# The 3 MB table of the relative bias written ahead of the values' projection instead of in the attention's set-up

## The chip, the cores and the metric

One core of one Trainium2 chip runs one decoder layer for a prompt group (2048 tokens) and a sample group (8 sequences, one token each). The metric is device microseconds of one execution; the kernel before takes 2285.19 us (median of 3 runs, 2283.89 to 2285.52). TensorE does matrix products, ScalarE and VectorE elementwise work, GpSimd some of it; SyncE (SP) does nothing but issue transfers. In this kernel transfers are issued by SP (they run on DMA queue 1) and by ScalarE (queue 10).

## The reference, cut to what matters

```python
h    = x * (1 + scale) + shift                    # scale, shift, gate from silu(c) @ w_ada
u_s, z_s, q, k, v, z_a, g_s, g_a = split(h @ w_in)
b_s  = (glu(gelu(S5(u_s))) * silu(z_s)) @ w_branch_s
s    = q . k / 8 + rel_bias[bucket(distance)]     # 16 heads, window of 128, masked outside
o    = softmax(s with a sink per head) @ v
b_a  = (o * silu(z_a)) @ w_branch_a
m    = sigmoid(g_s) * b_s + sigmoid(g_a) * b_a
y    = layer_norm(alpha * x + gate * (m @ w_out))
```

The bias depends only on the head and on the distance of query and key (0 to 128). The same formula runs for the 8 sample tokens against a cache of 128 keys and values, which is also returned, shifted by one.

## The kernel before, in words

Activations lie transposed, channels on the partitions, tokens along the free axis in five chunks of 512, 512, 512, 256 and 264 columns (the last holds the 8 sample tokens). A float32 product is made of three matmuls on split operands (high with high, high with low, low with high; L78). Weight columns come 128 at a time: SP loads them into `wst` (L55), ScalarE makes `whi` (L58), VectorE `wlo` (L59). A job is one such block times five chunks; each chunk is accumulated over 8 slices of 128 channels in one of three PSUM buffers `acc`, then copied out through one of two buffers with the tag `ev` and stored to DRAM.

The program runs in stages. Phase 1 (from about 20 to 332 us of the profiled span) makes u and the tables of the state-space branch, then in a pool `p1z` the first two blocks of z_a (the copies-out store to `zaP` by SP, L550) with the gate's small matmuls between them, and last `v_proj` (L648): the values, tokens on the partitions, in 17 tiles of up to 128 tokens. Each tile is 24 matmuls of 256 columns into an `acc` buffer (L665), a copy by ScalarE to `vt` in an `ev` buffer (L668), and a store to `vD` issued by ScalarE (L670). So three PSUM buffers and two `ev` buffers stand between TensorE and the stores. After it SP issues two copies of the sample caches to the outputs, about 1 MB each (`out_sk`, `out_sv`, L645). Phase 2 runs the scan of the state-space branch beside projection jobs.

Phase 3 begins near 903 us with `attn_setup` (L883), beside a projection job (`zr`, stored to `zsD` by ScalarE, L586 and L587). It builds the bias: a one-hot matrix times `rel_bias` gives 129 values for each of 16 heads (`pr`), VectorE puts them into `fr`, sixteen partitions of 384 columns that are -1e30 outside, and one transfer writes `fr` 128 times over into `biasD` in DRAM, 16 x 128 rows of 1536 bytes, 3072 KB (L895). Read back with a row length of 383, that is the band of biases of a block of queries (L1002). The set-up then does the whole attention of the sample tokens: scores, softmax (L864; the exponentials on ScalarE are L876 and L877), a transpose of the probabilities `t1s` (L940), products with the cached values (L954). The loop over the prompt's blocks (`attn_blocks`) follows, and is the first to read `biasD`. Phases 4 and 5 are the remaining products and the layer norm.

The code is written in stages, but a scheduler of the framework places each instruction on its engine's list; each engine then works its list in order. Every transfer tells its landing by one of eight semaphores in turn (`DMAHW0` to `DMAHW7` in the orders below), so that the ninth transfer waits for the first before it is issued.

Of the kernel before, what the change touches and what calls it, by code (L numbers as in the profile page):

```python
# [9 lines left out]
F32 = mybir.dt.float32  # L10
# [29 lines left out]
class Trunk:  # L40
# [576 lines left out]
    def phase1(self, ues, up):  # L617
        nc, I = self.nc, self.I
        w = I["w_in"][0]
        with ExitStack() as ses:  # L620
            self.sps = self.pool(ses, "sp1", 2, PSUM)
            with ues, ExitStack() as es:
                self.prp = self.pool(es, "prep")
                side = self.ssm_prep()
                jobs = []
                for m in range(1, 8):
                    b, e, f = self.u_job(up, m)
                    if m == 1:
                        def b(b=b, e=e):
                            b()  # L630
                            e(ORD[0], self.early)
                    jobs.append((self.cols(w, U0 + m * 128), e, b, f))
                self.products(jobs, self.X, self.cols(w, ZA0), self.every(3, side), first=ORD[1:])
                for _ in side:
                    pass
            with ExitStack() as es:
                p = self.pool(es, "p1z", 2)
                side = self.gate(p)
                self.products([self.za_job(m) for m in range(2)], self.X, self.cols(w, ZA0 + 256), self.every(2, side))
                for _ in side:  # L640
                    pass
                self.v_proj(p)
        for nm, src in (("sk", "cache_swa_k"), ("sv", "cache_swa_v")):
            self.tc.keep_in_program_order(
                nc.sync.dma_start(self.O[nm][0, :, 0:127].rearrange("b w g d -> b w (g d)"),  # L645
                                  I[src][0, :, 1:128].rearrange("b w g d -> b w (g d)")))
# [233 lines left out]
        for h in range(nh):  # L880
            v.tensor_scalar(t1[:, h, kw], t1[:, h, kw], den[:, h:h + 1], None, op0=OP.mult)

    def attn_setup(self, p, pp):  # L883
        nc, I = self.nc, self.I
        oh = p.tile([32, 129], F32, name="oh")
        nc.sync.dma_start(oh, I["c_onehot"])
        rb = p.tile([32, 16], F32, name="rb")
        nc.sync.dma_start(rb, I["rel_bias"])
        pr = pp.tile([16, 129], F32, name="pt", bufs=2)
        nc.tensor.matmul(pr, rb, oh, start=True, stop=True)  # L890
        fr = p.tile([16, 384], F32, name="fr")

        nc.vector.memset(fr, NEG)
        nc.vector.tensor_scalar(fr[:, 127:256], pr, 8.0, None, op0=OP.mult)
        nc.sync.dma_start(self.biasD.rearrange("h (r l) -> h r l", l=384), fr[:, None, :].to_broadcast([16, 128, 384]))  # L895

        rr = p.tile([32, NS, 16], F32, name="rr")
        nc.vector.tensor_copy(rr, rb[:, None, :].to_broadcast([32, NS, 16]))
# [532 lines left out]
```

## Time and profile before

| | |
|---|---|
| median of 3 runs | 2285.19 us |
| the profiled execution | 2281.77 us, its span 2280.0 us |
| TensorE busy | 2228.8 us, 98% |
| VectorE, ScalarE, GpSimd busy | 1464.8, 786.9, 349.7 us |
| DMA | 317.98 MB, 139 GB/s over the span |

The span runs from the first instruction to the last; all times within it count from its start. Busy shares are means over stages with different limits, so each stage is read by itself: which wait ends last there. L12 is line 12 of the kernel before.

### The profile page before, as it was taken

The numbers are of one execution on the slowest core, as the hardware profiler recorded it, in microseconds if no ns is written. First come the engines' busy times: TensorE is split into PE (matmuls) and PEld (weight loads), VectorE is DVE, ScalarE is ACT, GpSimd is POOL, SyncE is SP. The second block draws the span as 40 slices with busy tenths as digits, with TensorE's granted clock in tenths as the row PEclk, the third lists the DMA queues.
The fourth block names the chain that finished last, engine by engine and source line by source line (L and its number), as shares of the span: only waits on it lengthen the run. The fifth ranks groups of instructions, "written<-read, shape, count | busy, mean of one in ns | idle before, by whom it ended". The sixth has DMA issues, their size and how long they took to land.

```text
span 2280.0 us, 35059 instructions
## 1 busy us (share of the span) xinstructions
PE 2228.8 (98%) x12571; PEld 1904.1 (84%) x12571; DVE 1464.8 (64%) x3576; ACT 786.9 (35%) x1700; POOL 349.7 (15%) x420
## 2 busy tenths in 40 slices
PE   7999999999999999999999999999999999999998
PEld 5888798888888888788888888887877888888886
DVE  4896219998888883168998888546345115124887
ACT  3411213332111111167777667554234114112100
POOL 1100001111111111000000000014441000222232
PEclk9999999999999999999999999999999999999999
DMA  9344523334443343743334343477338447667431
GB/s 298 104 143 141 181 97 113 112 118 119 119 121 114 112 124 112 131 130 113 108 116 140 101 121 105 123 168 199 107 102 273 129 115 231 201 187 227 147 113 66
DMA packets 387502, 317.98 MB, mean 139 GB/s; under 512 B 89334, under 2 KB 331406, under 8 KB 385743
## 3 DMA queue, kind: packets, MB, share of 16 engines
q1 hardware_dynamic: 349616, 260.28, 40.3%
q10 hardware_dynamic: 37712, 55.47, 7.2%
q8 instruction: 99, 1.62, 0.3%
q14 instruction: 75, 0.61, 0.1%
HBM read 195.24 MB, written 122.63 MB: 139 GB/s over the span
## 4 chain that ended last, share of the span: by engine, by line
PE 80%; DMA 9%; DVE 4%; SPq 3%; issue 2%; ACT 1%; POOL 1%; POOLq 0%; DVEq 0%; ACTq 0%
PE acc L78 57%; PE po L1365 7%; DMA z<-zsD 3%; PE ps L1045 3%; PE po L1088 3%; PE pt L1072 2%; PE acc L665 2%; DMA biasD<-fr 2%; PE xp L784 1%; PE yp L817 1%; PE yp L816 1%; SPq L178 1%; DVE sg L1230 1%; DMA xst<-ozP 1%; DMA xst<-ysD 1%
## 5 line engine op out<-in xcount | busy, mean ns | idle before, releaser
L78 PE MATMUL acc<-hh,whi 128*128 128x512 f32 (+2 forms) x2000 | 712.6, 357 | 0.1
L78 PE MATMUL acc<-hl,whi 128*128 128x512 f32 (+2 forms) x2000 | 704.1, 352 | 0.0
L78 PE MATMUL acc<-hh,wlo 128*128 128x512 f32 (+2 forms) x2000 | 702.7, 351 | 0.2 <-DVE wlo L59 0.2
L78 PEld LDWEIGHTS acc<-hh,whi 128*128 128x128 f32 x2000 | 377.3, 189 | 49.1 <-issue 1.9
L78 PEld LDWEIGHTS acc<-hl,whi 128*128 128x128 f32 x2000 | 377.6, 189 | 48.5 <-issue 1.9
L78 PEld LDWEIGHTS acc<-hh,wlo 128*128 128x128 f32 x2000 | 377.4, 189 | 48.3 <-issue 1.0
L78 PE MATMUL acc<-xh,whi 128*128 128x512 f32 (+2 forms) x960 | 336.0, 350 | 14.6 <-ACT sg L1225 11.5
L78 PE MATMUL acc<-xl,whi 128*128 128x512 f32 (+2 forms) x960 | 334.7, 349 | 2.6 <-DVE xl L1172 2.5
L78 PE MATMUL acc<-xh,wlo 128*128 128x512 f32 (+2 forms) x960 | 333.4, 348 | 0.0
L78 PEld LDWEIGHTS acc<-xh,whi 128*128 128x128 f32 x960 | 181.5, 189 | 43.2 <-ACT sg L1225 15.8
L78 PEld LDWEIGHTS acc<-xl,whi 128*128 128x128 f32 x960 | 181.5, 189 | 27.3 <-DVE xl L1172 4.8
L78 PEld LDWEIGHTS acc<-xh,wlo 128*128 128x128 f32 x960 | 181.2, 189 | 23.1
L1172 DVE TENSOR_TENSOR xl<-xst,xh 128x1024 fp32r<-128x1024 f32 (+2 forms) x84 | 104.2, 1259 | 72.2 <-ACT xh L1171 71.8
L59 DVE TENSOR_TENSOR wlo<-wst,whi 128x1024 fp32r<-128x1024 f32 x74 | 94.7, 1280 | 76.1 <-ACT whi L58 75.4
L1059 ACT ACTIVATE t<-t,nm 128x256 f32<-128x256 f32 (+1 forms) x256 | 126.5, 496 | 46.4 <-DVE nm L1049 45.3
L58 ACT CAST whi<-wst 128x1024 fp32r<-128x1024 f32 x74 | 77.6, 1048 | 140.8 <-PE acc L78 130.0
L1099 POOL TENSOR_TENSOR o<-o,z 128x512 f32<-128x512 f32 x32 | 43.4, 1355 | 519.0 <-DVE o L1093 472.2
L1171 ACT CAST xh<-xst 128x1024 fp32r<-128x1024 f32 (+2 forms) x84 | 85.6, 1043 | 107.9 <-DMA xst<-mD 34.3
L1049 DVE CUSTOM_DVE_ANT_0 t<-ps,bias,skb 128x256 f32<-128x256 f32 (+1 forms) x256 | 109.7, 470 | 5.9 <-issue 3.1
L1365 PE MATMUL po<-wol,xh 128*128 128x512 f32 (+1 forms) x272 | 102.7, 377 | 0.8 <-DVE wol L1288 0.8
L586 ACT COPY zr<-acc 128x512 f32<-128x512 f32 (+2 forms) x120 | 59.4, 495 | 126.1 <-PE acc L78 91.6
L1365 PE MATMUL po<-woh,xh 128*128 128x512 f32 (+1 forms) x272 | 102.6, 377 | 0.0
(362 smaller groups left out, 3404.6 us busy)
## 6 DMA issues: line engine op xcount, KB each, us to landing
wst<-in_w_in SPq DMA_DIRECT2D x50, 512.0 KB
uD<-u ACTq DMA_DIRECT2D x8, 1088.0 KB
u<-uD SPq DMA_DIRECT2D x32, 272.0 KB
yD<-y ACTq DMA_DIRECT2D x64, 132.0 KB
x<-in_x_prompt SPq DMA_DIRECT2D x16, 512.0 KB
wa<-in_w_ada SPq DMA_DIRECT2D x16, 512.0 KB
qf<-qD SPq DMA_DIRECT2D x32, 256.0 KB
z<-zaP SPq DMA_DIRECT2D x32, 256.0 KB
```

The costliest lines, as they stand in the source:

```text
L58: nc.scalar.copy(hi, st)
L59: nc.vector.tensor_tensor(lo, st, hi, op=OP.subtract)
L78: self.nc.tensor.matmul(ps[:, :n], w[:, k, :], x[:, k, :], start=(k == 0 and i == 0), stop=(k == KT - 1 and i == 2))
L586: nc.scalar.copy(z[:, :n], ps[:, :n])
L665: nc.tensor.matmul(ps[:mt, :256], x[:, k, ts], w[:, k, :], start=(i == 0), stop=(i == 23))
L1045: nc.tensor.matmul(ps[:, a2, kw], s["q"][e][:, 2 * g + a2], kk[:, g, kw], start=(i == 0), stop=(i == 1))
L1049: v.tensor_tensor_reduce(t1[:, h, kw], ps[:, a2, kw], s["bias"][:, 4 * g + h, b0:b0 + kw.stop], -0.125, nsk[:, hs:hs + 1], OP.add, OP.min, ...
L1059: nc.scalar.activation(t1[:, h, kw], t1[:, h, kw], AF.Exp, bias=nm[:, h:h + 1], scale=-1.0, accum_out=den[:, h:h + 1])
L1088: nc.tensor.matmul(pr, s["v"][h][:, g], x.rearrange("p a q -> p (a q)"), start=(h == hs[0] and i == 0), stop=(h == hs[-1] and i == 1))
L1171: nc.scalar.copy(xv(hi[:, k - 1:k + 1]), sv(st))
L1172: nc.vector.tensor_tensor(xv(lo[:, k - 1:k + 1]), sv(st), xv(hi[:, k - 1:k + 1]), op=OP.subtract)
L1365: nc.tensor.matmul(ps[:, :w], X[a][:, k, ts], Wo[h * w // 512][b][:, k, ws], start=(i == 0), stop=(i == 23))
```

## The change

The one-hot product, the filling of `fr` and the write of `biasD` move out of `attn_setup` into a new function `bias_rows`, called in phase 1 between the gate and `v_proj`. The write is issued by ScalarE instead of SP, `fr` comes from the pool `p1z`, and the product goes to a buffer of phase 1's small PSUM pool. The loads of the one-hot matrix and of `rel_bias` are made twice, since the set-up still needs them for the sample tokens.

```diff
@@ -639,6 +639,7 @@
                 self.products([self.za_job(m) for m in range(2)], self.X, self.cols(w, ZA0 + 256), self.every(2, side))
                 for _ in side:
                     pass
+                self.bias_rows(p, self.sps)
                 self.v_proj(p)
         for nm, src in (("sk", "cache_swa_k"), ("sv", "cache_swa_v")):
             self.tc.keep_in_program_order(
@@ -880,19 +881,28 @@
         for h in range(nh):
             v.tensor_scalar(t1[:, h, kw], t1[:, h, kw], den[:, h:h + 1], None, op0=OP.mult)
 
+    def bias_in(self, p):
+        oh = p.tile([32, 129], F32, name="oh", bufs=1)
+        self.nc.sync.dma_start(oh, self.I["c_onehot"])
+        rb = p.tile([32, 16], F32, name="rb", bufs=1)
+        self.nc.sync.dma_start(rb, self.I["rel_bias"])
+        return oh, rb
+
+    def bias_rows(self, p, pp):
+
+        nc = self.nc
+        oh, rb = self.bias_in(p)
+        pr = pp.tile([16, 129], F32, name="tr")
+        nc.tensor.matmul(pr, rb, oh, start=True, stop=True)
+        fr = p.tile([16, 384], F32, name="fr", bufs=1)
+
+        nc.vector.memset(fr, NEG)
+        nc.vector.tensor_scalar(fr[:, 127:256], pr, 8.0, None, op0=OP.mult)
+        nc.scalar.dma_start(self.biasD.rearrange("h (r l) -> h r l", l=384), fr[:, None, :].to_broadcast([16, 128, 384]))
+
     def attn_setup(self, p, pp):
         nc, I = self.nc, self.I
-        oh = p.tile([32, 129], F32, name="oh")
-        nc.sync.dma_start(oh, I["c_onehot"])
-        rb = p.tile([32, 16], F32, name="rb")
-        nc.sync.dma_start(rb, I["rel_bias"])
-        pr = pp.tile([16, 129], F32, name="pt", bufs=2)
-        nc.tensor.matmul(pr, rb, oh, start=True, stop=True)
-        fr = p.tile([16, 384], F32, name="fr")
-
-        nc.vector.memset(fr, NEG)
-        nc.vector.tensor_scalar(fr[:, 127:256], pr, 8.0, None, op0=OP.mult)
-        nc.sync.dma_start(self.biasD.rearrange("h (r l) -> h r l", l=384), fr[:, None, :].to_broadcast([16, 128, 384]))
+        oh, rb = self.bias_in(p)
 
         rr = p.tile([32, NS, 16], F32, name="rr")
         nc.vector.tensor_copy(rr, rb[:, None, :].to_broadcast([32, NS, 16]))
```

On ScalarE at the start of `v_proj`, before (`z` is the last tile of z_a; `vt` and `vD` as above; in brackets the engines and the DMA semaphores that an instruction waits for):

```order
L546 ACTIVATE z_3090<-acc_3065 128x512 [waits DMAHW6_49,DVE_49,PE_49]
L668 COPY vt_3125<-acc_3100 128x256 [waits DMAHW1_49,PE_49,Pool_49]
L670 DMA vD_102<-vt_3125 128x256 [waits DMAHW4_49,Activation_49]
L668 COPY vt_3153<-acc_3128 128x256 [waits DMAHW3_49,DVE_49,PE_49]
L670 DMA vD_102<-vt_3153 128x256 [waits DMAHW5_49,Activation_49]
L668 COPY vt_3181<-acc_3156 128x256 [waits DMAHW4_49,PE_49]
L670 DMA vD_102<-vt_3181 128x256 [waits Activation_49]
L668 COPY vt_3209<-acc_3184 128x256 [waits DMAHW5_49,PE_49]
```

and after:

```order
L546 ACTIVATE z_3090<-acc_3065 128x512 [waits DMAHW0_49,DVE_49,PE_49]
L901 DMA biasD_104<-fr_3100 2048x1x384 [waits DMAHW2_49,DVE_49]
L669 COPY vt_3135<-acc_3110 128x256 [waits DMAHW1_49,PE_49,Pool_49]
L671 DMA vD_102<-vt_3135 128x256 [waits DMAHW7_49,Activation_49]
L669 COPY vt_3163<-acc_3138 128x256 [waits DMAHW6_49,DVE_49,PE_49]
L669 COPY vt_3191<-acc_3166 128x256 [waits DMAHW7_49,PE_49]
L671 DMA vD_102<-vt_3163 128x256 [waits Activation_49]
L671 DMA vD_102<-vt_3191 128x256 [waits Activation_49]
L669 COPY vt_3219<-acc_3194 128x256 [waits DMAHW0_49,PE_49]
L671 DMA vD_102<-vt_3219 128x256 [waits DMAHW2_49,Activation_49]
```

The write stands ahead of all copies and stores of the values, and the third copy now precedes the second store. The write takes semaphore 2 of the eight, which the fourth store of `vD` waits for.

On SP at the same place, before:

```order
L550 DMA zaP0_153<-z_3031 128x512 [waits DMAHW6_49,DVE_49]
L645 DMA out_sk<-in_cache_swa_k 8x2x16256 [waits DMAHW7_49]
L645 DMA out_sv<-in_cache_swa_v 8x2x16256 [waits DMAHW0_49]
L550 DMA zaP0_153<-z_3060 128x264 [waits DMAHW1_49,DVE_49]
L55 DMA wst_3972<-in_w_in 128x8x128 [waits DMAHW2_49,DVE_49]
L550 DMA zaP0_153<-z_3090 128x512 [waits DMAHW3_49,DVE_49]
```

and after:

```order
L550 DMA zaP0_153<-z_3031 128x512 [waits DMAHW0_49,DVE_49]
L550 DMA zaP0_153<-z_3060 128x264 [waits DMAHW1_49,DVE_49]
L646 DMA out_sk<-in_cache_swa_k 8x2x16256 [waits DMAHW3_49]
L646 DMA out_sv<-in_cache_swa_v 8x2x16256 [waits DMAHW4_49]
L55 DMA wst_3982<-in_w_in 128x8x128 [waits DMAHW5_49,DVE_49]
L550 DMA zaP0_153<-z_3090 128x512 [waits DMAHW6_49,DVE_49]
```

The store of the last but one z tile has moved ahead of the two copies of the caches; the weights `wst` and the last z store stay behind them.

On ScalarE in the attention's set-up, around the sample softmax, before (`zr` and `zsD` are the projection job's):

```order
L586 COPY zr_9451<-acc_9382 128x256 [waits DMAHW0_49,PE_49]
L587 DMA zsD5_110<-zr_9451 128x256 [waits DMAHW3_49,Activation_49]
L586 COPY zr_9512<-acc_9460 128x512 [waits DMAHW2_49,PE_49]
L587 DMA zsD5_110<-zr_9512 128x512 [waits DMAHW4_49,Activation_49]
L876 ACT_TABLE_LOAD [waits DMAHW6_49,DMAHW1_49]
L876 ACTIVATE t1s_9004,den_9167<-t1s_9004,nm_9163 128x129 [waits DVE_49]
L877 ACTIVATE es_9165<-es_9165 128x1 [waits DVE_49]
```

and after:

```order
L586 COPY zr_9455<-acc_9386 128x256 [waits DMAHW2_49,PE_49]
L587 DMA zsD5_110<-zr_9455 128x256 [waits DMAHW5_49,Activation_49]
L586 COPY zr_9516<-acc_9464 128x512 [waits DMAHW4_49,PE_49]
L587 DMA zsD5_110<-zr_9516 128x512 [waits DMAHW6_49,Activation_49]
L877 ACT_TABLE_LOAD
L877 ACTIVATE t1s_9008,den_9171<-t1s_9008,nm_9167 128x129 [waits DVE_49]
L878 ACTIVATE es_9169<-es_9169 128x1 [waits DVE_49]
```

The table load ahead of the exponential waited for two transfers, of which semaphore 6 is the one that the write of `biasD` used; it now waits for none. VectorE's and TensorE's lists lose the few instructions of the product there and keep the rest in order.

## Rows read from the trace of the kernel before

**Rows 1.** The page: engines' busy time, and the chain that ended last by line.
```profile
PE 2228.8 (98%) x12571; PEld 1904.1 (84%) x12571; DVE 1464.8 (64%) x3576; ACT 786.9 (35%) x1700; POOL 349.7 (15%) x420
...
PE acc L78 57%; PE po L1365 7%; DMA z<-zsD 3%; PE ps L1045 3%; PE po L1088 3%; PE pt L1072 2%; PE acc L665 2%; DMA biasD<-fr 2%; PE xp L784 1%; PE yp L817 1%; PE yp L816 1%; SPq L178 1%; DVE sg L1230 1%; DMA xst<-ozP 1%; DMA xst<-ysD 1%
```

**Rows 2.** The chain of waits, 860 to 1010: start us, us, what.
```profile
909.08 36.17 DMA biasD<-fr
...
945.27 1.28 ACT L876
```

**Rows 3.** Timeline of TensorE: start us, us, instruction [idle before, releaser].
```profile
942.47 0.39 PE L78 MATMUL acc<-hl,whi 128*128 128x512 f32 x1
948.01 0.45 PE L940 MATMUL pt<-ident,t1s 128*128 128x128 f32 x1 [5.15 <-DVE t1s L881]
...
949.32 0.63 PE L78 MATMUL acc<-hl,whi 128*128 128x512 f32 x1
949.75 0.63 PE L78 MATMUL acc<-hh,wlo 128*128 128x512 f32 x1
...
951.45 0.40 PE L78 MATMUL acc<-hh,whi 128*128 128x512 f32 x1
951.68 0.40 PE L78 MATMUL acc<-hl,whi 128*128 128x512 f32 x1
```

**Rows 4.** Stretches: us, busy of each engine, granted clock, DMA share, GB/s.
```profile
948.00:950.00 2.00, 1.99 (x6) 1.63 (x7) 0.48 (x2) 1.06 (x2) 0.00 (x0) 0.50 0.23 80
950.00:952.00 2.00, 2.00 (x7) 1.53 (x7) 1.23 (x1) 0.85 (x2) 0.00 (x0) 0.64 0.21 79
```

**Rows 5.** Timeline of ScalarE ahead of the sample softmax.
```profile
936.76 0.37 ACT L586 COPY zr<-acc 128x256 f32<-128x256 f32 x1 [8.46 <-DMA zsD<-zr]
...
944.22 0.58 ACT L586 COPY zr<-acc 128x512 f32<-128x512 f32 x1 [7.09 <-DMA zsD<-zr]
```

**Rows 6.** Timeline of VectorE, the softmax's last input.
```profile
936.59 0.15 DVE L871 TENSOR_SCALAR nm<-mxs 128x1 f32<-128x1 f32 x1
```

**Rows 7.** DMA of 914 to 940: packets; then queue, packets, MB, share.
```profile
DMA packets 1883, 2.87 MB, mean 110 GB/s; under 512 B 32, under 2 KB 1734, under 8 KB 1882
...
q1 hardware_dynamic: 1574, 2.42, 85.7%
q10 hardware_dynamic: 308, 0.44, 5.1%
```

**Rows 8.** DMA of 906 to 912, queue 1.
```profile
q1 hardware_dynamic: 1770, 1.80, 91.4%
```

**Rows 9.** Timeline of SP, which issues DMAs.
```profile
909.08 0.67 SPq L895 DMA_DIRECT2D biasD<-fr  x1
918.14 33.88 SPq L55 DMA_DIRECT2D wst<-in_w_in  x2
```

**Rows 10.** Waits of SP, 905 to 955: in total, times, longest us.
```profile
SPq L55 <- DMA wst<-in_w_in: 27.8, 1, 27.8
```

**Rows 11.** Timeline of ScalarE at the start of v_proj.
```profile
284.13 0.59 ACT L546 ACTIVATE z<-acc 128x512 f32<-128x512 f32 x1
...
291.65 0.33 ACTq L670 DMA_DIRECT2D vD<-vt  x1
...
294.31 0.37 ACT L668 COPY vt<-acc 128x256 f32<-128x256 f32 x1 [0.45 <-ACT vt L668]
...
297.81 0.37 ACT L668 COPY vt<-acc 128x256 f32<-128x256 f32 x1 [1.77 <-PE acc L665]
...
300.69 0.37 ACT L668 COPY vt<-acc 128x256 f32<-128x256 f32 x1 [2.51 <-PE acc L665]
```

**Rows 12.** Line 665: matmuls, duration ns, first and last start.
```profile
L665 PE MATMUL acc<-vh,hh x136: 276/281/285, 283.2 to 331.6; 128*128 128x256 f32 x128, 128*8 128x256 f32 x8
```

**Rows 13.** Timeline of SP at the start of v_proj.
```profile
285.51 0.39 SPq L55 DMA_DIRECT2D wst<-in_w_in  x1
286.11 1.58 SPq L550 DMA_DIRECT2D zaP<-z  x1
```

## The prediction

> **What bounds the kernel now.** The page comes first: TensorE is busy 98% of a span of 2280.0 us, and the chain that ended last is mostly L78 matmuls [rows 1]. So a move of DMA work pays only where TensorE itself stands still, and costs as soon as it makes TensorE stand still elsewhere. The chain of waits around the table's write shows the one place where the write is on the path: it runs from the issue of biasD at 909.08 for 36.17 us straight to ScalarE's L876 (the exponential of the sample group's softmax) and from there to TensorE's L940 [rows 2]. TensorE's timeline gives the loss: it has worked through to 942.86 (942.47 plus 0.39), then is idle for 5.15 us until 948.01 [rows 3]. Afterwards the granted clock is 0.50 of full speed from 948 to 950, which is the lower level of 1.2 GHz, and 0.64 in the mean of the next two [rows 4].
>
> **What is removed.** The stall goes. In the order of ScalarE before, L876 waits for two DMA semaphores, one of them the one that biasD uses; after, it waits for none. The two zr copies queued ahead of it on ScalarE were themselves held 8.46 and 7.09 us by zsD stores that crawled beside the write [rows 5]. Without the write the softmax's last input is ready on VectorE at 936.74 [rows 6]; from the table load to the transpose the chain took 945.27 to 948.01, 2.74 us [rows 2, 3], so t1s would stand near 939.5, some 3 us ahead of the moment (942.86) when TensorE asks for it. Gain: 5.15 us idle. On top, 512-column matmuls start 0.43 us apart until 951.45 and 0.23 us apart from there [rows 3]: of the 3.44 us from 948.01 on the lower clock cost 3.44 x (1 - 0.23/0.43) = 1.6 us. Together 6.7 us. What is late next there: nothing on the trace before L954. The bounds on this term: 0 if kc and vc (2 MB, issued just ahead of the write) delay the softmax by themselves, 6.7 if not; I take 6.7, since the wait names the write.
>
> **What is added at the new place.** Two loads (oh, rb), one small matmul, a memset and a scaling, and the 3 MB write itself on ScalarE's DMA queue, ahead of the values' projection. The loads (2 and 16 KB) stand on SP ahead of vst, which is not needed before v_proj begins at 283.2 [rows 12]: nothing. The matmul, one of 129 columns, leaves the set-up as it comes in here: nothing. In the set-up the two loads and the rr path stay.
>
> The write is the term that decides. How long it takes is read where it stood: between 914 and 940 queue 1 moved 1574 packets of 2.42 MB, 1537 bytes each, with 85.7% of sixteen engines [rows 7]. These are the table's rows of 1536 bytes and nothing else: 0.857 x 16 x 26 / 1574 = 0.227 us a packet. All 2048 of them need 2048 x 0.227 / 16 = 29.0 us of every engine, or 33.8 us at the occupation of that stretch. The cheapest comparable row: in 906 to 912, kc and vc go at 1770 packets of 1.80 MB with 91.4%, 0.050 us for 1017 bytes, which is 0.075 us for 1536 and 9.6 us for the table [rows 8]. The dearest: 36.17 us from issue to end [rows 2]. The source is the same tile of sixteen partitions in both kernels, so I take 29 to 34, not 9.6. The Trainium skill, SBUF — State Buffer, section on the DMA port swizzle, puts partitions 0 to 15 on four of sixteen ports, a quarter of about 435 GB/s; an estimate from that page is 28.9 us for 3.15 MB. The trace agrees with that pace (1537 bytes in 0.227 us on sixteen engines is 108 GB/s), so the slowness would travel with the tile.
>
> What is queued behind it: a wst load was issued on the same queue at 918.14 [rows 9], but no packet of 512 bytes is among the 1574 up to 940 [rows 7], and SP's next issue waited 27.8 us for it, until 946.3 [rows 10], one us after the write's end. So one queue serves its transfers in order. After the change the write is on ScalarE's queue, and behind it are the vD stores of v_proj. ScalarE issues it after the last z activation, 284.13 + 0.59 = 284.7 [rows 11]. With about 2 us to start and 29 to 33.8 us of moving it ends between 315.8 and 320.6; the two copies out_sk and out_sv, which in the new order stand behind one more zaP store on SP, still run at that time and make the late half likelier. I take 318.
>
> Now the wait. A vt copy needs one of two ev buffers: vt0 and vt1 those of the last z tiles, vt2 the one of vt0, free when vD0 has landed. Before, that was 294.31, 2.66 us after vD0's issue at 291.65 [rows 11]. After, vD0 lands behind the write, about 319. Accumulators in PSUM are three. TensorE starts v_proj at 283.2 [rows 12] and needs 2.88 us a tile (297.81 to 300.69, [rows 11]), so tile 4 starts at 294.8 and tile 5 at 297.7. If vt1 is copied in time, TensorE stops at tile 5 and goes on at about 319.5 (vt2 copied in 0.37): 21.8 us. The new order of ScalarE puts vD1's store behind vt2's copy, so that vt3 waits one more landing (2.66 us); TensorE is at tile 5 for 2.88, so that adds at most half a us. If vt1 is not in time it stops at tile 4. vt1 needs the zaP store issued at 286.11, which stands on queue 1 behind a 512 KB wst load from 285.51 [rows 13]. While the write ran, the other queue got 308 packets in 26 us [rows 7], but wst (1024 runs of 128 columns) and zaP (128 of 512 columns) are 1152; at that pace they land only after the write, at about 320.5, and TensorE goes on at 321: 26.2 us. The Trainium skill, DMA: Bandwidth & Descriptors, section on queues and rings, says that each engine takes turns between the queues, packet by packet; by that rule queue 1 would get half the turns, vt1 would come early, and the stall would be the 21.8. The row of 308 in 1883 speaks for less than half. I take 24 us between the two.
>
> What hides it: nothing. TensorE takes its matmuls in order, and behind tile 4 or 5 on its queue there is only the rest of v_proj and then phase 2. After the stall the clock costs again what it did at 948: 1.6 us. Everything after it is shifted as a whole: phase 2 is TensorE-bound, and its loads are issued by SP behind the wait for vD. Bounds of the stall: 0 (the write at kc's pace ends at 297) to 29 (36.17 us after issue, vt1 last).
>
> **Sum.** +24 + 1.6 - 6.7 = +18.9 us. On the profiled execution (2281.77 us, 1.8 us around its span) that is 2300.7; that execution is 3.4 us below the median of 2285.19, which is what I forecast from: 2304.
>
> **Rivals.**
> - The write is cheap at the new place: v_proj's stores are small and few, and either overtake it or the write runs at kc's pace. Then only the gain stays: 2285.2 - 6.7 = 2278.5, faster. For it: v_proj itself asks for no more than one 128 KB store per 2.88 us. Against it: 0.227 us a packet with hardly anything beside it.
> - The stores on the same queue do overtake, but the fourth vD store waits on the semaphore that biasD used (the order shows it): ScalarE stops there, TensorE at tile 7 (303.5) until 319: 15.5 + 1.6 - 6.7 = +10.4, 2295.6. Against it: the wst that did not overtake.
> - The stall comes as forecast, but the gain doesn't, because kc and vc or zsD hold the softmax: 24 + 1.6 = +25.6, 2310.8. For it: kc and vc remain; against it: they are done by 914, 22 us before the softmax.
> - The change does little: the write ends near 304, so that a stall of some 5 us pays back the gain: 2285. It needs half the packet time.
>
> **How the numbers follow.** Forecast (stall 20 to 29 us) 0.70, own range 2300 to 2309; cheap write 0.07; fourth store 0.08; gain missing 0.08; evens out 0.07. A change of 0.2% (4.6 us) is about what a measurement tells here. Slower 0.70 + 0.08 + 0.08 = 0.86, same 0.07, faster 0.07. The range 2291 to 2313 takes in the fourth store and the missing gain.
>
> **What would show it.** Right: TensorE idle between about 295 and 320 in L665, its releaser the vt copies and behind these a DMA of vD or zaP; half clock for some 3 us after; the chain through biasD there; no idle before the sample transpose; queue 10 with the 1536-byte packets at about 0.22 us. Wrong: L665 without a gap (the first rival), a gap from 303 (the second), an idle at the sample transpose still (the third).

## The result, and the profile after

The change made the kernel slower: 2306.27 us (median of 6, 2301.89 to 2312.44) beside 2284.54 us for the kernel before in the same rounds (median of 6, 2282.39 to 2285.99), ratio 1.0101, interval 1.0091 to 1.0111. The profiled execution took 2305.43 us, its span 2303.7 us. Line numbers of v_proj are one higher than before (L666 the matmuls, L669 the copy of `vt`, L671 the store of `vD`), the write is L901.

The table of waits of TensorE names the loss: its longest entry has no counterpart before. The 5.15 us at the sample softmax [rows 3], which stood in the list before, have gone from it. Columns: who waited and for whom, us in total, times, longest.

```profile
PE acc L666 <- ACT vt L669: 25.1, 1, 25.1
...
PE yp L817 <- DMA tt<-tD: 3.0, 4, 1.3
```

TensorE's timeline has the stop, 25.15 us ahead of the fifth tile. The matmuls follow 0.21 us apart until 325.93 and 0.11 us apart from there:

```profile
319.79 0.58 PE L666 MATMUL acc<-vh,hh 128*128 128x256 f32 x1 [25.15 <-ACT vt L669]
...
325.72 0.41 PE L666 MATMUL acc<-vh,hh 128*128 128x256 f32 x1
325.93 0.33 PE L666 MATMUL acc<-vl,hh 128*128 128x256 f32 x1
326.09 0.28 PE L666 MATMUL acc<-vh,hl 128*128 128x256 f32 x1
```

The windows give the granted clock (the column before the DMA share): 0.50, which is 1.2 GHz, until after 324, and all of 2.4 GHz from 328.

```profile
320.00:324.00 4.00, 4.00 (x19) 4.00 (x20) 0.00 (x0) 0.37 (x1) 0.00 (x0) 0.50 0.28 64
324.00:328.00 4.00, 4.00 (x28) 4.00 (x28) 0.00 (x0) 0.74 (x2) 0.00 (x0) 0.75 0.30 101
328.00:332.00 4.00, 4.00 (x38) 4.00 (x37) 0.00 (x0) 0.74 (x2) 0.00 (x0) 1.00 0.11 37
```

ScalarE's timeline of the same place answers to [rows 11]. Besides the copies it shows its issues (ACTq):

```profile
283.89 0.70 ACTq L901 DMA_DIRECT2D biasD<-fr  x1
...
286.56 0.37 ACT L669 COPY vt<-acc 128x256 f32<-128x256 f32 x1 [1.99 <-PE acc L666]
286.96 13.70 ACTq L671 DMA_DIRECT2D vD<-vt  x1
319.37 0.37 ACT L669 COPY vt<-acc 128x256 f32<-128x256 f32 x1 [32.43 <-DMA zaP<-z]
322.75 0.37 ACT L669 COPY vt<-acc 128x256 f32<-128x256 f32 x1 [3.02 <-DMA vD<-vt]
...
358.62 0.36 ACT L669 COPY vt<-acc 8x256 f32<-8x256 f32 x1 [2.35 <-PE acc L666]
```

Three things stand there. The second copy, vt1, waited until 319.37 for the last store of z; the third, vt2, for the first `vD` store, which landed at about 322.7. And the issue of that store alone, 0.33 us before, held ScalarE for 13.70 us, which nobody had forecast. SP's store `zaP<-z` was issued at 285.96, behind `wst`:

```profile
285.36 0.40 SPq L55 DMA_DIRECT2D wst<-in_w_in  x1
285.96 3.66 SPq L550 DMA_DIRECT2D zaP<-z  x1
```

The DMA queues from 296 to 316 (packets, MB, share of sixteen engines), to be read beside [rows 7]:

```profile
q10 hardware_dynamic: 1236, 1.90, 87.1%
q1 hardware_dynamic: 898, 0.56, 9.3%
```

A packet of the table takes 0.871 x 16 x 20 / 1236 = 0.226 us, as it did in the set-up (0.227).

The gain is read best from two marks on TensorE: the last scores of the sample group and the first product with the cached values. Before:

```profile
934.65 1.05 PE L931 MATMUL po<-kts,qm 128*128 128x129 f32 x8
...
954.76 0.64 PE L954 MATMUL po<-vc,pTs 128*32 128x256 f32 x8
```

After, with the sample transpose (L950) standing between them without idle time:

```profile
963.35 1.05 PE L941 MATMUL po<-kts,qm 128*128 128x129 f32 x8
...
971.53 0.27 PE L950 MATMUL pt<-ident,t1s 128*128 128x128 f32 x1
...
976.66 0.64 PE L964 MATMUL po<-vc,pTs 128*32 128x256 f32 x8
```

The way between the marks shrank from 20.11 to 13.31 us: 6.8 us given back. The first mark stands 28.7 us later than before, the second 21.9 us. Behind it the profiled execution loses 1.8 us more (its span is 23.7 us longer); the medians differ by 21.7 us.

### The profile page after: what moved, and what is told of

It reads as the page before. It is cut to its first block, busy times and chain, and to the rows that moved or that the text cites. A ratio compares the mean times of both kernels' runs of the same rounds, so it can differ in the third digit from the quotient of the medians.

```text
span 2303.7 us, 35061 instructions
## 1 busy us (share of the span) xinstructions
PE 2229.7 (97%) x12571; PEld 1904.9 (83%) x12571; DVE 1464.9 (64%) x3576; ACT 786.8 (34%) x1700; POOL 347.7 (15%) x420
## 5 line engine op out<-in xcount | busy, mean ns | idle before, releaser
L1375 PE MATMUL po<-woh,xl 128*128 128x512 f32 (+1 forms) x272 | 102.7, 378 | 0.0
```

Source lines behind the costliest of these rows:

```text
L1375: nc.tensor.matmul(ps[:, :w], X[a][:, k, ts], Wo[h * w // 512][b][:, k, ws], start=(i == 0), stop=(i == 23))
```

## The experiments

Every kernel was timed beside the kernel before; the ratio with its interval is against that.

**e1: the kernel after, with the source on 128 partitions.** Each head's row is made on eight partitions, so that the write reads 128 partitions instead of sixteen.

```diff
-        pr = pp.tile([16, 129], F32, name="tr")
-        nc.tensor.matmul(pr, rb, oh, start=True, stop=True)
-        fr = p.tile([16, 384], F32, name="fr", bufs=1)
+        r8 = p.tile([32, 16, 8], F32, name="r8", bufs=1)
+        nc.vector.tensor_copy(r8, rb[:, :, None].to_broadcast([32, 16, 8]))
+        pr = pp.tile([128, 129], F32, name="tr")
+        nc.tensor.matmul(pr, r8.rearrange("b h a -> b (h a)"), oh, start=True, stop=True)
+        fr = p.tile([128, 384], F32, name="fr", bufs=1)
...
-        nc.scalar.dma_start(self.biasD.rearrange("h (r l) -> h r l", l=384), fr[:, None, :].to_broadcast([16, 128, 384]))
+        nc.scalar.dma_start(self.biasD.rearrange("h (a r l) -> (h a) r l", a=8, l=384), fr[:, None, :].to_broadcast([128, 16, 384]))
```

Expected: 

> The changed kernel, but the filled rows stand on 128 partitions (8 copies of each head's row, made by a one-hot product with 8 times repeated columns) and each partition writes 16 rows; same place, same queue, same destination, same 1536-byte rows. Theory A (the write is slow because sixteen partitions feed it, and v_proj's stall is the length of the write): a packet falls from 0.22 us to 0.08 to 0.11, the write lasts 10 to 15 us, v_proj's stall falls from 25.1 us to 2 to 6, and the time is 2279 to 2285 against 2306 of the changed kernel and 2284.5 of the one before. Rival B (the rows of 1536 bytes or the destination in DRAM set the pace): packets stay at 0.22, stall 25, time 2306.

Measured: 2285.9 us, ratio 1.0006 (0.9996 to 1.0015), 0.9 us above theory A's range. Its waits of TensorE and ScalarE's timeline:

```profile
PE acc L666 <- ACT vt L669: 5.4, 1, 5.4
```

```profile
286.95 7.76 ACTq L671 DMA_DIRECT2D vD<-vt  x1
299.56 0.37 ACT L669 COPY vt<-acc 128x256 f32<-128x256 f32 x1 [12.65 <-DMA zaP<-z]
```

Same bytes, same place, same queue; the stall falls from 25.1 to 5.4 us, and the time by 20 us. So most of the loss hangs on the time that the write takes. The place still costs something: v_proj ends 6.6 us later than before (its last copy starts at 338.72 against 332.14), which the gain in the set-up about pays back, and e2, with the same source at the old place and timed in the same rounds, is 10.4 us faster.

**e2: the kernel before, with the same source.** The same edit in the attention's set-up; the write stays there, on SP.

Expected: 

> The kernel before, the write left in the attention's set-up on SP's queue, but from 128 partitions as in the run above. Theory A: the write ends some 20 us earlier, near 925, the stores of zsD go back to about 3 us, ScalarE reaches the sample softmax in time, and TensorE's 5.15 us ahead of the sample transpose and the 1.6 us of lower clock behind it are gone: 2277 to 2279 against 2284.5. Rival B: packets stay at 0.22 us, the stall stays, 2284.5. Rival C (kc and vc hold the softmax, not the write): the packets are fast but the stall stays, 2284.

Measured: 2275.53 us, ratio 0.9966 (0.9956 to 0.9976), 1.5 us below theory A's range. Queue 1 from 918 to 924, and ScalarE's exponential:

```profile
q1 hardware_dynamic: 1489, 2.29, 100.8%
```

```profile
938.66 1.28 ACT L876 ACT_TABLE_LOAD   x1 [0.39 <-ACT zr L586]
```

The table's packets take 1.008 x 16 x 6 / 1489 = 0.065 us instead of 0.227. The exponential's table load waits for no DMA any more, and stands at 938.66 instead of 945.27 [rows 2]. So the gain that the change was to bring is had without moving the write, and v_proj has no stop. This is the fastest version of all that ran, and beats both kernels.

**e3: the kernel after, with four buffers of its own for vt.** Takes away the waits of the copies for earlier stores, but not the issue.

```diff
-                vt = self.ev.tile([128, 256], F32, name="vt", tag="ev")
+                vt = p.tile([128, 256], F32, name="vt", bufs=4)
```

Expected: 

> The changed kernel, with four buffers of its own for vt in place of the two shared with the z tiles. Theory A: the write is as long as before, four tiles can be copied out and three stand in PSUM, so TensorE stops not at tile 4 (294.6) but at tile 7, near 303, and goes on when the stores behind the write land, near 318 to 320: stall 14 to 17 us, time 2295 to 2299. Rival D (the stall comes from the zaP store alone, and the stores of vD would pass the write on their queue): no wait for a landing but the fourth store's semaphore; were that not so late either, no stall and 2279. Rival E (TensorE is slowed by the write itself, not by buffers): 2306.

Measured: 2297.43 us, ratio 1.0062 (1.0047 to 1.0077). TensorE's stops:

```profile
301.10 0.58 PE L666 MATMUL acc<-vh,hh 128*128 128x256 f32 x1 [6.56 <-ACT vt L669]
...
309.36 0.38 PE L666 MATMUL acc<-vh,hh 128*128 128x256 f32 x1 [0.72 <-ACT vt L669]
...
324.02 0.58 PE L666 MATMUL acc<-vh,hh 128*128 128x256 f32 x1 [11.68 <-ACT vt L669]
```

and ScalarE's timeline:

```profile
286.82 13.81 ACTq L671 DMA_DIRECT2D vD<-vt  x1
300.68 0.37 ACT L669 COPY vt<-acc 128x256 f32<-128x256 f32 x1 [13.89 <-issue]
...
308.93 0.37 ACT L669 COPY vt<-acc 128x256 f32<-128x256 f32 x1 [3.43 <-PE acc L666]
323.18 0.33 ACTq L671 DMA_DIRECT2D vD<-vt  x1
```

The time is as forecast, by way of a stop that was not: with its buffer free, vt1 waits for nothing but ScalarE, and that stands 13.81 us in the issue of a store. The stops come to 19.0 us in all, where 14 to 17 were expected. The fourth store is issued at 323.18, 14 us after its copy, and has the semaphore of the write, as in the prediction's second rival; here it wasn't ScalarE's last wait, for the copy behind it (323.60) waited for the first `vD` store.

**e4: the kernel after, with the write issued by SP.**

```diff
-        nc.scalar.dma_start(self.biasD.rearrange("h (r l) -> h r l", l=384), fr[:, None, :].to_broadcast([16, 128, 384]))
+        nc.sync.dma_start(self.biasD.rearrange("h (r l) -> h r l", l=384), fr[:, None, :].to_broadcast([16, 128, 384]))
```

Expected: 

> The changed kernel, with the write issued by SP on its queue instead of by ScalarE. The stores of vD then have their queue to themselves; out_sk, out_sv, wst and the last zaP store stand behind the write. Theory A (what TensorE waits for is a buffer whose store lands after the write, here the zaP store that vt1 needs): vt1 is free only when the write (till about 316), the two copies, wst and zaP are done, near 325: stall 28 to 33 us, time 2308 to 2316. Rival D (the stores of vD behind the write on one queue are the whole stall): no stall, 2279.

Measured: 2313.31 us, ratio 1.013 (1.0115 to 1.0145); the stall is 36.4 us (expected: 28 to 33), its releaser again vt1 behind the zaP store. SP's timeline:

```profile
284.16 0.65 SPq L901 DMA_DIRECT2D biasD<-fr  x1
284.87 9.32 SPq L646 DMA_DIRECT2D out_sk<-in_cache_swa_k  x1
294.23 4.57 SPq L646 DMA_DIRECT2D out_sv<-in_cache_swa_v  x1
...
303.11 17.33 SPq L550 DMA_DIRECT2D zaP<-z  x1
```

The held issue goes with the queue of the write: now SP's issues last 4 to 17 us each, while ScalarE's `vD` store is issued in 0.33 us. What stands behind the write on its queue pays, whichever queue that is. The store on the other queue had to wait as well: issued at 287.24, it moved nothing up to 298 (from 285 to 298 queue 1 has 797 packets and queue 10 none).

**e5: the kernel before, with an extra write.** A second table of the same size goes to a spare place in DRAM ahead of v_proj on ScalarE's queue (`bias_rows` as in the change, writing `biasE`), and the set-up keeps its own write. This is the loss without the gain.

```diff
+        self.biasE = dp.tile([16, 128 * 384], F32, name="biasE")
...
+                self.bias_rows(p, self.sps)
                 self.v_proj(p)
...
```

Expected: 

> The kernel before, with a second write of the same table (into a spare place in DRAM that nobody reads) ahead of v_proj on ScalarE's queue; the set-up keeps its own write, on SP. So the added part alone. Theory A (the loss is the write at the new place: 25.1 us of stall and 3.1 us of lower clock, and the set-up's gain of some 7 us is separate from it): TensorE idle 24 to 26 us in v_proj behind the vt copies, the 5 us at the sample transpose still there, 2283.3 + 28 = 2309 to 2314. Theory B (the stall comes in part from the new order of SP and ScalarE that goes with the removed part): stall under 22 us and a time under the 2306 of the kernel after.

Measured: 2313.04 us, ratio 1.0123 (1.0102 to 1.0143), 27.9 us above the kernel before in its rounds. TensorE's waits have both entries:

```profile
PE acc L667 <- ACT vt L670: 25.3, 1, 25.3
...
PE pt L955 <- DVE t1s L883: 5.3, 1, 5.3
```

So the loss is the added part alone (27.9 us) and the gain is what the set-up gives back (27.9 - 21.7 = 6.2 us by the medians, 6.8 us by the marks above; the interval leaves the 27.9 some 5 us either way). The two add up, as the prediction's sum had it.

**e6 and e7: the write behind v_proj.** The call of the table's part stands after v_proj instead of ahead of it; e7 has the 128 partitions of e1 besides. No `vD` store is behind the write then.

```diff
-                self.bias_rows(p, self.sps)
                 self.v_proj(p)
+                self.bias_rows(p, self.sps)
```

Expected of e6: 

> The kernel after with the table's part called behind v_proj instead of ahead of it: the write is still in phase 1, still on ScalarE's queue and from sixteen partitions, but no vD store stands behind it. Theory A (the loss hangs on what is queued behind the write, not on the write): no idle in v_proj, gain of the set-up kept, 2277 to 2281 if phase 2's first loads bear the write beside them. Theory B (30 us at sixteen slow partitions hurt whoever loads beside them): phase 2's first pairs wait for pk, u and tD, up to 15 us, 2284 to 2292.

Expected of e7: 

> As the one before, with the table's source on 128 partitions (packets of 65 ns, write of some 10 us in all). Theory A: no wait in v_proj, none at the sample transpose, hardly any in phase 2: 2274 to 2278, the level of the kernel before with 128 partitions (2275.5). Theory B: half or more of the late write's price in phase 2 stays: 2280 or more.

Measured: e6 2306.4 us, ratio 1.0094 (1.0076 to 1.0112); e7 2288.18 us, ratio 1.0016 (1.0004 to 1.0028). Both miss their theory A. e6 lies above the range of its theory B too; e7 falls under its theory B (2280 or more). In e6 v_proj has no stop, but phase 2 begins with these:

```profile
PE tr L746 <- DVE bt L719: 8.9, 1, 8.9
PE yp L817 <- DMA tt<-tD: 8.1, 7, 2.1
PE acc L78 <- DVE z L547: 6.4, 2, 3.8
```

and SP's timeline there tells a part of the reason: the two copies of the caches and two zaP stores now stand ahead of phase 2's first load, `pk`.

```profile
332.87 0.75 SPq L646 DMA_DIRECT2D out_sk<-in_cache_swa_k  x1
...
339.47 4.49 SPq L550 DMA_DIRECT2D zaP<-z  x2
344.06 3.69 SPq L706 DMA_DIRECT2D pk<-packD  x1
347.85 4.31 SPq L697 DMA_DIRECT2D tD<-zt  x1
```

In the kernel before `pk` is issued at 332.17; here at 344.06, and the issues beside the write last about 4 us each. The longest of the waits, 8.9 us, hangs on the write itself. SP's waits and VectorE's timeline show it:

```profile
SPq L698 <- DMA biasD<-fr: 14.7, 1, 14.7
```

```profile
377.35 0.69 DVE L739 TENSOR_TENSOR tm<-pk 128x512 f32<-128x512 f32 x1 [9.07 <-DMA tD<-zt]
```

The last of four stores that fill the margins of `tD` with zeros (L698) touches nothing of the table, but has the semaphore of the write in the trace, so that SP waits 14.7 us for the write to land. `tm`, which takes the buffer of these zeros, waits for that store, and `bt` and TensorE wait for `tm`. In e7 `pk` comes at 342.20, about as late, but the issues behind it last 0.4 us, and TensorE loses only 9.7 us, to `tt`. For the rest the runs don't tell the late write apart from the order of SP that came with it; what they show is that 3 MB at the slow pace cost 18 us more (2306.4 against 2288.18) than at the fast one here too, and that neither run found the end of phase 1 a free place for it.

**e8: the kernel after, with the two copies of the caches issued some 40 us earlier.** I held that their large packets kept the last zaP store back.

```diff
+            for nm, src in (("sk", "cache_swa_k"), ("sv", "cache_swa_v")):
+                self.tc.keep_in_program_order(
+                    nc.sync.dma_start(self.O[nm][0, :, 0:127].rearrange("b w g d -> b w (g d)"),
+                                      I[src][0, :, 1:128].rearrange("b w g d -> b w (g d)")))
             with ExitStack() as es:
                 p = self.pool(es, "p1z", 2)
...
-        for nm, src in (("sk", "cache_swa_k"), ("sv", "cache_swa_v")):
...
```

Expected: 

> The kernel after, with the two copies of the sample caches (out_sk, out_sv) issued some 40 us earlier, so that queue 1 has only wst and the last zaP store beside the write. Theory A (the queues take turns by packet; zaP was late because the copies' packets of 65 KB held half the engines): vt1 is copied when ScalarE's held issue of vD0 is over, near 301; TensorE stops for 6 to 7 us at tile 4, and again at tile 5 until vD0 has landed behind the write, near 317; together 19 to 22 us, 2300 to 2303. Theory B (the write's queue gets far more than half the turns, whatever else runs): zaP lands only with the write's end, one stall of 24 to 26 us, 2305 to 2308.

Measured: 2310.71 us, ratio 1.0107 (1.0083 to 1.013). v_proj begins 7 us later, of which 3.9 are TensorE's waits for the gate's weights, now issued behind the copies (the rest was not traced), and the stall is 25.8 us, one piece, behind zaP as before: theory A of this run falls. The queues from 292 to 305, from the write's first packet on, and with `wst` issued at 292.39 on a queue that had nothing else:

```profile
q10 hardware_dynamic: 816, 1.25, 86.4%
...
q1 hardware_dynamic: 3, 0.00, 0.0%
```

and from 305 to 321:

```profile
q10 hardware_dynamic: 1000, 1.54, 88.3%
q1 hardware_dynamic: 896, 0.46, 9.5%
```

For some 12 us the other queue gets hardly a turn; then it gets almost one for one. Both halves cost here: `wst` is 1024 packets, 64 on each engine, and a turn of each queue lasts 0.883 x 16 x 16 / 1000 = 0.226 us for the table's packet and 0.027 us for wst's, so 64 turns last 16 us. Then comes zaP.

**e9: the kernel after, with two buffers of its own for vt.** As e3, with `bufs=2`: vt1 is free of zaP, vt2 still waits for the first `vD` store.

Expected: 

> The kernel after, with vt in two buffers of its own instead of the two that it shares with z: so vt1 no longer waits for the last zaP store, but vt2 still for vD0. Theory A (two waits end nearly together, the zaP store behind wst, and vD0 behind the write): TensorE stops for 6 to 7 us at tile 4, as ScalarE is held in vD0's issue until 301, and at tile 5 from 304 to 318 to 320; together 20 to 23 us, of which 2 to 5 us are won against the 25.1 us of the kernel after; 2302 to 2305. Theory B (zaP is what costs, vD0 lands early): stall under 12 us, 2295 or less.

Measured: 2302.35 us, ratio 1.0077 (1.006 to 1.0093). TensorE's stops:

```profile
301.78 0.58 PE L666 MATMUL acc<-vh,hh 128*128 128x256 f32 x1 [6.54 <-ACT vt L669]
...
324.08 0.58 PE L666 MATMUL acc<-vh,hh 128*128 128x256 f32 x1 [16.81 <-ACT vt L669]
```

As theory A had it: 23.3 us in two pieces, the second released at 323.65 by the `vD` store. The two waits behind the write end within a few us of each other, so that taking one away buys only 4 us.

## Why the prediction was right, step by step

The forecast was 2304 us, the range 2291 to 2313; the time is 2306.27. On the profiled execution the terms stand so:

| term | forecast | measured |
|---|---|---|
| stall in v_proj | 24 (21.8 or 26.2) | 25.15 |
| lower clock after it | 1.6 | 2.7 |
| faster tiles in v_proj (the rest of the 26.5 us at its end) | 0 | about -1.4 |
| from there to the sample scores | 0 | +2.2 |
| set-up | -6.7 | -6.8 |
| sum, up to the second mark | +18.9 | +21.9 |

- **The write keeps its pace.** Right for the pace: 0.226 us a packet at the new place. The write ended somewhat later than I took, though: `vD0`, which stands behind it, landed at about 322.7 and not at 319; from 284 to 290 the two copies of the caches had moved 1.24 MB beside its start, which the prediction had named as a risk. The cheap write (2278.5) falls by the pace. The Trainium skill, SBUF — State Buffer, section on the DMA port swizzle, makes the partitions the cause; e1 and e2 bear that out, with 0.065 us for the same packet from 128 partitions.
- **The stall, its place and its releaser.** Right: of the two cases it was the dearer, vt1 late, TensorE stopped at tile 4 (idle from 294.64), 25.15 against 26.2 us. The estimate of 24 was taken between the two and lay 1.1 us short. The cheaper case was priced too low, since `vD0` was late as well: e9, in which vt1 doesn't wait for zaP, still stops for 23.3 us.
- **Why vt1 is late.** Half right. I argued from the 308 packets in 26 us [rows 7] that the other queue gets far less than half the turns. It got 898 against 1236 (296 to 316), and in e8 one for one, but only after some 12 us with hardly a turn. The Trainium skill, DMA: Bandwidth & Descriptors, section on queues and rings, has the engines take turns by packet; after those 12 us the trace agrees with it; why the 12 us pass without turns no run shows. What I drew from that rule was wrong: even with full turns zaP is late, since every small packet waits for one slow one. An estimate: the 1152 packets are 72 for each of sixteen engines, and 72 turns of 0.253 us (e8) are 18 us, so from the first `wst` packets near 291 zaP would land near 309. That it landed at 319 takes the lost turns besides. So the dearer case came with only half of its reason, which is in part luck. Queue 10 in [rows 7] fits this: it wasn't short of work, for the copies of `zr` waited 8.46 and 7.09 us for stores that had been issued and had not landed [rows 5].
- **What is queued behind the write.** Right, and more than I saw: the stores land behind it, and their issue holds the engine that issues them (13.70 us of ScalarE). It didn't set the end here, since zaP and vD were later still; in e3 and e9 it made a stop of 6.5 us of its own. A small sign of it stood in the trace before: the first `wst` behind the write took 3.04 us to issue (918.14 to 921.18), the next one 0.37. The 33.88 us of [rows 9] are these two with the wait of [rows 10] between them. So I had that wait's end wrong as well: 921.18 + 27.8 is 949.0 and not 946.3.
- **The fourth store's semaphore (2295.6).** Didn't decide here: the stop came three tiles earlier. The mechanism is real, for in e3 the fourth store and in e6 a store of zeros stood behind the write in this way.
- **The lower clock.** Mis-sized. TensorE was at 1.2 GHz for 6.1 us after the stop (319.79 to 325.93), where it had been 3.44 us after the stop at 948; at 0.120 us a matmul, the pace of v_proj before (2.88 us for 24), that costs 6.14 x (1 - 0.120/0.213) = 2.7 us and not 1.6.
- **The gain.** Right, 6.8 against 6.7 us, with e2 as a second witness: 13.18 us between the same two marks (938.45 to 951.63) instead of 20.11, and 2275.53 against 2283.3 us in its rounds. The rival in which kc and vc hold the softmax (2310.8) falls.
- **Phase 2 as a mere shift.** Not quite: 26.5 us of delay at the end of v_proj (358.62 against 332.14) had become 28.7 at the sample scores. The waits for `tt` rose from 0.3 to 3.0 us; why was not tried. They vary without the move: e2, whose edit lies behind phase 2 in the program, has 4.3 us of them, e3 0.9. So the 2.2 us are not shown to come from the move.
- **What would show it.** One sign could not be read: the chain that ended last starts at about 1575 us in the profile after, so it doesn't reach back to the write.

## What to carry to other kernels

Before a long transfer is moved away from a stall, ask why it is long: here sixteen source partitions made 3 MB take 29 us or more, and spreading the source over 128 bought at the old place (ratio 0.9966) all that the move was to buy. Where a transfer must be moved, price it by what stands behind it on its queue and on the engine that issues, and what the other queue's small packets need when each waits for a slow one: two or three such waits end together, and removing one shows the next. An issue that lasts 13 us, where others last 0.3, is a price, not an oddity; but a merged row (x2) is taken apart first, as the 33.88 us of [rows 9] show, nearly all of which was a wait. And a transfer with nothing to do with the long one can still wait for its landing, by the semaphore that the two share (e6).

## What the runs showed of the hardware that was not expected

- Issuing behind a long transfer on the same queue holds the issuing engine: 13.70 us for one store (after), 7.76 us where the write is fast (e1), up to 17.33 us on SP (e4); 3.04 us where the write had been under way for 9 us (the kernel before, 918.14). On the other queue an issue lasted 0.33 us at the same time (e4), though zaP's lasted 3.66 us in the kernel after (1.58 before [rows 13]).
- A transfer that is issued on the other queue just behind the write can go without turns for over 10 us (e8: 3 packets against 816 from 292 to 305, 51 of the write for each engine; e4: none against 797 from 285 to 298), as if these packets had been handed to the engines already. In the kernel after `wst` came as soon behind the write and moved its first packets between 290 and 292, but in proportions of about a half (319 to 547, 292 to 300), one (479 to 481, 300 to 308) and a half again (267 to 503, 308 to 316), as if half the engines had begun at once and half some 9 us later. The trace doesn't tell the engine of a packet; this was not tried.
- In the kernel after most tiles of v_proj take 2.72 us, in the kernel before 2.88, at a granted clock of 1.00 in both. The stall is not the cause, since the pace is there ahead of it (the second of these is 24 matmuls behind the first):

```profile
290.06 0.28 PE L666 MATMUL acc<-vh,hh 128*128 128x256 f32 x1
...
292.78 0.28 PE L666 MATMUL acc<-vh,hh 128*128 128x256 f32 x1
```

  All runs that make the table ahead of v_proj are faster than the kernel before there (2.72 us in e1, e3, e5 and e9, 2.83 in e4 and e8); e6 and e7, which make it behind, have 2.88. The cause stays open.
